# Gate and up expert weights fetched in 8 KB runs, with the normed tokens stored block by block to match

## The chip, the cores and the metric

The kernel runs on one core of one Trainium2 chip. The metric is the device time of one execution in microseconds, the median of several runs. All numbers are float32, or float32r, which is float32 as TensorE reads it in its faster form.

## What is computed

Two transformer blocks in a row work on 256 tokens of width 1024. The first has gated delta-rule attention, differential attention and a dense feed-forward part; the second has a mixer, cross attention to a memory, and a mixture of 32 experts. The change touches the last part alone:

```
h   = rmsnorm(x) * g_moe                       # 256 tokens x 1024
top-1 of 4 groups, top-2 of the 8 experts in it, per token
out = sum over the chosen experts e of  weight[e] * (silu(h @ Wg[e]) * (h @ Wu[e])) @ Wd[e]
x   = rmsnorm(x + out) * g_final
```

Wg and Wu are 1024 x 512 for each expert, Wd is 512 x 1024: 2 MB each, 6 MB for an expert, 192 MB in all. Every expert has 64 slots for tokens. A second pass for experts with more tokens than that lies behind an If at the end.

## The kernel before

**The stage.** Everything up to the router takes some 636 us. Then the expert stage, `moe` (L2045), goes through the 32 experts in 16 pairs. The two experts of a pair sit side by side in halves of TensorE's columns, 64 slots each.

**The weights.** `Experts` (L341) loads the weights on SP's queue in units of 1 MB into slots of 8 KB for each of the 128 partitions. An expert has six units: q = 0 to 3 for gate and up, q = 4 and 5 for down. The order (L347 to 349) is gate and up of pair 0; then, for each p up to 13, gate and up of pair p + 1 and down of pair p; then down of pair 14, gate and up of pair 15, down of pair 15. There are 22 slots: 4 from the time of the first block's feed-forward part (`NRE`), 5 from the time of the cross attention (`NRT`), and 13 more when the buffers of the earlier stages come free (L803). Early on one unit is loaded behind each weight block of the earlier stages (`S.after`, L790 and L795); in `moe` the loads are issued by `X.load` (L2050, L2195, L2212, L2214), as far as slots come free. The list of units goes round the slots, so unit i waits for the last reader of unit i - 22.

**A fetch.** `fetch` (L357) makes a gate/up unit out of two transfers of 512 KB, 256 rows of gate and 256 of up. Partition p takes rows 2p and 2p + 1 of the 256, which lie side by side in memory, 4 KB in one run. A down unit is one transfer of 256 rows of 4 KB; partition p takes rows 2p and 2p + 1, 8 KB in one run.

**The tokens to match.** Since a partition holds rows 2p and 2p + 1, the feature blocks that are multiplied by them are every second feature of 256. `gather` (L2071) multiplies the tokens by one-hot matrices and so collects the tokens of each slot, feature by slot, in `xe`; it reads every second column of x with a step of two (L2079). The columns of `gm`, by which the result is scaled (L2083), are packed in that order on the host (L125). Pair 0 gathers from x itself; the later pairs gather from `xh` and `xl`, two parts of the normed tokens that add up to them (written at L2188 to L2192), four experts at a time.

**The order of a pair.** A turn of the loop (L2198) has: `gather` in even turns; `hid_T`, which transposes the hidden values of pair p; `one_hot`; `gate_up` of pair p + 1; `down` of pair p. `gate_up` (L2097) goes through feature block k, gate or up c, expert j, with one product `mm` (two instructions) for each. Behind the first eight products it calls `between`, which holds `combine` (adds the outputs of pair p - 1 to the tokens) and `slots_T`. `evac` (L2121) takes a pair's output from TensorE's banks, on ACT and VectorE.

```
for k, c, j in [(k, c, j) for k in range(8) for c in range(2) for j in range(n)]:
    if between and (k, c, j) == (2, 0, 0):
        between()
    self.mm(g[c][H[j]], xe[:, k, j0 + j], ws_(j, k // 2)[:, c, k % 2], k == 0, k == 7)
```

**The planner.** In the earlier stages the order of the work is written out by `drive`, which advances the chain that `Pace` (L149) holds to be ready first. `Pace.note` books a transfer by its bytes and an operation by its elements. The router (L1834) is one of the chains. The expert stage is written out by hand.

Of the kernel before, what the change touches and what calls it, by code (L numbers as in the profile page):

```python
# [18 lines left out]
F32 = mybir.dt.float32  # L19
F32R = mybir.dt.float32r  # L20
I32 = mybir.dt.int32
AF = mybir.ActivationFunctionType
ALU = mybir.AluOpType
# [8 lines left out]
CAP = 64  # L32
# [59 lines left out]
def colmajor(v):  # L92
    v = np.asarray(v)
    return v.reshape(-1, 128).T


def pack_small(I):
    g = lambda n: np.asarray(I[n])
    P = Pack()
    P.add("attn_norm", colmajor(g("attn_norm_w")[0]))  # L100
    P.add("ffn_norm", colmajor(g("ffn_norm_w")[0]))
    P.add("g_mix", colmajor(g("g_mix_2")[0]))
    P.add("g_cross", colmajor(g("g_cross_2")[0]))
    P.add("g_moe", colmajor(g("g_moe_2")[0]))
    P.add("g_mem", colmajor(g("g_mem_2")))
    P.add("conv", g("conv_w")[0].reshape(4, 12, 128).transpose(2, 1, 0))
    P.add("la_norm", g("la_norm_w")[0].reshape(128, 1))
    P.add("diff_norm", g("diff_norm_w")[0].reshape(128, 1))
    P.add("gla_norm", g("g_gla_head_2")[0].T)
    P.add("lam_q", np.stack([g("lambda_q1")[0], g("lambda_q2")[0]], 1))  # L110
    P.add("lam_k", np.stack([g("lambda_k1")[0], g("lambda_k2")[0]], 1))
    P.add("a_log", np.broadcast_to(g("a_log")[0], (128, 4)))
    P.add("dt_bias", np.broadcast_to(g("dt_bias")[0], (128, 4)))
    ba = np.zeros((1024, 8), np.float32)
    ba[:] = g("w_in")[0][:, 2048:2056]
    P.add("w_ba", ba.reshape(8, 128, 8).transpose(1, 0, 2))
    P.add("w_alr", g("w_in_2")[0][:, 1536:1552].reshape(8, 128, 16).transpose(1, 0, 2))
    P.add("w_alpha", np.concatenate([g("w_alpha_up_2")[0], g("b_alpha_2")[0][None]], 0))
    rb = np.concatenate([g("rel_bias"), g("rel_bias_2")], 1)
    P.add("rel_bias", np.concatenate([rb, np.ones((1, 12), np.float32)], 0))  # L120
    wr = np.concatenate([g("w_router_group_2")[0], g("w_router_expert_2")[0]], 1)
    P.add("w_rt", wr.reshape(8, 128, 36).transpose(1, 0, 2))
    P.add("b_rt", np.broadcast_to(np.concatenate([g("b_router_group_2")[0], g("b_router_expert_2")[0]]), (128, 36)))
    P.add("final_norm", colmajor(g("final_norm_w")))
    P.add("g_moe_rows", g("g_moe_2")[0].reshape(4, 128, 2).transpose(1, 0, 2))  # L125
    return P


# [141 lines left out]
class Stream:  # L270
# [17 lines left out]
    def load(self, upto=RAW):  # L288
        while self.loaded < len(self.units) and self.loaded < self.freed + upto:
            src, k, n = self.units[self.loaded]  # L290
            w = self.raw[self.loaded % RAW].rearrange("p (k n) -> p k n", n=n)
            src = src.rearrange("(k p) n -> p k n", p=128)
            step = k if self.loaded else 1
            for i in range(0, k, step):
                self.K.nc.sync.dma_start(w[:, i:i + step], src[:, i:i + step])
            self.loaded += 1
            self.after()
# [43 lines left out]
class Experts:  # L341
# [12 lines left out]
        new = [pool.tile([128, 2048], F32, name=f"wm{i}") for i in range(len(order))]  # L354
        self.slots += [new[i] for i in order]

    def fetch(self, slot, e, q, cut=False):  # L357

        nc, I = self.K.nc, self.K.I
        one = (lambda w: w[0, e]) if isinstance(e, int) else (lambda w: w[0, e, :, :].rearrange("o k n -> (o k) n"))  # L360
        rows = lambda n, q: one(I[n])[q * 256:(q + 1) * 256, :].rearrange("(p k) n -> p k n", k=2)
        if q < 4:
            w = slot.rearrange("p (c k n) -> p c k n", k=2, c=2)
            for c, name in enumerate(("w_exp_gate_2", "w_exp_up_2")):
                nc.sync.dma_start(w[:, c], rows(name, q))
        else:
            w = slot.rearrange("p (k n) -> p k n", k=2)
            src = rows("w_exp_down_2", q - 4)
            if cut:
                return w, src  # L370
            nc.sync.dma_start(w, src)
        return w

    def load(self, upto):
        upto = min(upto, len(self.slots)) if self.early else upto
        while self.n < min(upto, len(self.order) - 2):
            self.units[self.order[self.n]] = self.fetch(self.slot(self.n), *self.order[self.n])
            self.n += 1
        if self.n == len(self.order) - 2 and upto >= len(self.order):
            two = [self.fetch(self.slot(self.n + i), *self.order[self.n + i], True) for i in range(2)]  # L380
            for c in range(2):
                for w, src in two:
                    self.K.nc.sync.dma_start(w[:, :, c * 512:c * 512 + 512], src[:, :, c * 512:c * 512 + 512])
            for i, (w, _) in enumerate(two):
                self.units[self.order[self.n + i]] = w
            self.n += 2
# [35 lines left out]
class K:  # L422
# [131 lines left out]
    def rows(self, o, x, k, t, hi, lo, first, last):  # L554
        a = slice(t * 128, (t + 1) * 128)
        self.mm(o, x.hi(k)[:, a], hi, first, False)
        self.mm(o, x.hi(k)[:, a], lo, False, False)
        self.mm(o, x.lo(k)[:, a], hi, False, last)
# [1275 lines left out]
    def router(self, done, ss):  # L1834

        nc = self.nc
        V = nc.vector
        R = self.rt
        self.gm = R.tile([128, 8], F32, name="gm")
        nc.gpsimd.tensor_copy(self.gm, self.small("g_moe_rows"))  # L1840
        hT = [self.g1([128, 2, T], "hT") for _ in range(4)]
        wr = self.small("w_rt").rearrange("p (k n) -> p k n", n=36)
        yield 0
# [2 lines left out]
        for n in range(2):  # L1846
# [3 lines left out]
            for k in range(4 * n, 4 * n + 4, 2):  # L1850
                bank = yield from self.take()
                b = bank.rearrange("p (k n) -> p k n", k=2)
# [82 lines left out]
        while gens[0] or gens[1]:  # L1935
            for i in range(2):
                if gens[i]:
                    try:
# [8 lines left out]
        b = yield from self.take()  # L1947
        strict, one = self.const("strict"), self.ones
# [10 lines left out]
                               op0=ALU.add, op1=ALU.mult)  # L1959
# [85 lines left out]
    def moe(self, A):  # L2045
        tc, nc, I = self.tc, self.nc, self.I
        V = nc.vector
# [3 lines left out]
        x, rk, W32, one_hot, col = self.x, self.rk, self.W32, self.one_hot, self.col  # L2051
        NP = NE // 2
        H = [slice(0, CAP), slice(CAP, 2 * CAP)]
# [5 lines left out]
        xh = [A.tile([128, D], F32R, name=f"xh{t}") for t in range(2)]  # L2059
        xl = [A.tile([128, D], F32R, name=f"xl{t}") for t in range(2)]  # L2060
        xe = self.xe
# [6 lines left out]
                            ranks[:, :, :, None].to_broadcast([128, 2, n, CAP]), op=ALU.is_equal)  # L2068
            return oh

        def gather(n, oh, parts, j0=0, ds=range(8)):  # L2071


            per = 4 if n <= 2 else 2
            for d0 in ds[::per]:
                b = self.bank()[:, :per * n * CAP].rearrange("p (d s) -> p d s", d=per)
                for d in range(per):
                    q, i = (d0 + d) // 2, (d0 + d) % 2
                    mms = [(xs[t][:, q * 256:(q + 1) * 256].rearrange("p (m i) -> p i m", i=2)[:, i], t)  # L2079
                           for t in range(2) for xs in parts]  # L2080
                    for m, (w, t) in enumerate(mms):
                        self.mm(b[:, d], w, oh[:, t, :n].rearrange("p e s -> p (e s)"), m == 0, m == len(mms) - 1)
                V.tensor_tensor(xe[:, d0:d0 + per, j0:j0 + n].rearrange("p d e s -> p d (e s)"), b,  # L2083
                                self.gm[:, d0:d0 + per, None].to_broadcast([128, per, n * CAP]), op=ALU.mult)

        def slots_T(n, pw):

# [9 lines left out]
        def gate_up(n, j0, ws_, between=None):  # L2097

            g = [self.bank() for _ in range(2)]
            for k, c, j in [(k, c, j) for k in range(8) for c in range(2) for j in range(n)]:  # L2100
                if between and (k, c, j) == (2, 0, 0):
                    between()
                self.mm(g[c][H[j]], xe[:, k, j0 + j], ws_(j, k // 2)[:, c, k % 2], k == 0, k == 7)
            sg = self.sg
            R = slice(0, n * CAP)
            nc.scalar.activation(sg[R], g[0][R], AF.Silu)
            V.tensor_tensor(sg[R], g[1][R], sg[R], op=ALU.mult)
            return sg
# [75 lines left out]

        unit = lambda p: (lambda j, q: X.units[2 * p + j, q])
        quad = lambda p: rk[:, :, 2 * p:min(2 * p + 4, NE)]
        gather(2, self.oh, [x])
        for t in range(2):  # L2188
            nc.scalar.activation(xh[t], x[t], AF.Copy, scale=self.r[:, t:t + 1])
        oh = hot(quad(1), 4)  # L2190
        for t in range(2):
            V.scalar_tensor_tensor(xl[t], x[t], self.r[:, t:t + 1], xh[t].bitcast(F32), op0=ALU.mult, op1=ALU.subtract)  # L2192
        hd = gate_up(2, 0, unit(0))
        ys = [[y[:, i] for i in range(2)] for y in (self.c.tile([128, 2, 512], F32R, name=f"ys{c}", tag=f"x{c}") for c in range(2))]
        X.load(8 + NR)  # L2195
# [2 lines left out]
        for p in range(NP - 2):  # L2198
# [4 lines left out]
            if p % 2:  # L2203
                oh = hot(quad(p + 2), min(4, NE - 2 * (p + 2)))
# [11 lines left out]
        p = NP - 2  # L2216
# [20 lines left out]
        with tc.If(most > CAP):  # L2237
            with tc.For_i(0, NE, 1) as e:
                one = bass.ds(e, 1)
# [5 lines left out]
                for _ in range(1, T // CAP):  # L2245
# [4 lines left out]
                    for c in range(2):  # L2250
                        for t in range(2):
                            b = self.bank()
# [34 lines left out]
```

## Time and profile before

| | |
|---|---|
| Runs | 1098.84 us median of three (1098.18 to 1101.12) |
| Profiled execution | 1100.28 us, of it 1098.5 us from the first to the last instruction (the span) |
| Busy share of the span | PE 97%, PEld (weight loads) 68%, DVE 46%, ACT 35%, POOL 5% |
| Chain that ended last, by engine | PE 73%, DMA 21%, DVE 2%, ACT 2%, issue 1% |
| Moved by DMA | 300.06 MB in 106462 packets, mean 273 GB/s |
| Gate, up transfers | 128 each, 512 KB, 10.2 us from issue to landing |
| Down transfers | 62 of 1 MB, 12.6 us, and 4 of 512 KB, 12.7 us |
| Mean granted clock of TensorE | 0.995 |

PE is TensorE, DVE is VectorE, POOL is GpSimd; SP only issues transfers here. A busy PE is not yet a PE at its peak, since matmuls are pipelined and their ends are modelled. The chain of waits is followed back from the last instruction to whatever released each step. All instructions carry one line, L249, that of a helper that records them, so groups are told apart by the names of the tiles: `wm` are the expert slots, `xe` the gathered tokens, `sg` and `hdT` the hidden values, `ys` the outputs of a pair, `ohr` and `oh` the one-hot matrices, `pwT` the matrix that `combine` uses.

### The profile page before, as it was taken

The page shows a single profiled execution, that of the slowest core. Times are in us where ns is not written, and L with a number is a line of the kernel's source. Part 1 is how long each engine was busy: PE and PEld are TensorE (multiplying, and loading weights), DVE is VectorE, ACT ScalarE, POOL GpSimd, SP SyncE. Part 2 cuts the span into 40 slices and gives each one's busy share as a digit, 9 for nine tenths or more (in the row PEclk, how much of TensorE's full clock was granted, in tenths as well). Part 3 has the DMA queues.
Part 4 walks back from the last instruction along what each step waited for, and adds up shares of the span by engine and source line. Part 5 has one row for each costly group of instructions (what it writes and reads, how often), then busy time and mean ns, then how long its engine had stood idle before and what let it go on. Part 6 is the DMA issues. An engine that isn't in the chain of part 4 may idle for free.

```text
span 1098.5 us, 16788 instructions
## 1 busy us (share of the span) xinstructions
PE 1062.1 (97%) x6848; PEld 747.5 (68%) x6848; DVE 504.0 (46%) x917; ACT 381.1 (35%) x678; POOL 57.3 (5%) x85
## 2 busy tenths in 40 slices
PE   9999999999999999999999999999999988989896
PEld 8989788999999888889998753434343434333252
DVE  5777746665655667666576442212121212121021
ACT  6553546644444475566446411000000000000012
POOL 0154011000000010100000000000000000000000
PEclk9999999999999999999999999999999999999998
DMA  8354115576556445454469789999999999999993
GB/s 307 120 190 128 59 66 173 202 271 218 176 170 204 159 136 182 146 178 150 161 217 388 267 314 413 413 414 412 413 414 412 412 412 412 414 412 414 416 413 150
DMA packets 106462, 300.06 MB, mean 273 GB/s; under 512 B 6999, under 2 KB 35980, under 8 KB 98444
## 3 DMA queue, kind: packets, MB, share of 16 engines
q1 hardware_dynamic: 104924, 294.71, 71.3%
q0 software_dynamic: 1024, 3.17, 1.0%
q8 instruction: 56, 0.92, 0.3%
q10 hardware_dynamic: 432, 1.05, 0.3%
q14 instruction: 26, 0.21, 0.1%
HBM read 297.83 MB, written 1.07 MB: 272 GB/s over the span
## 4 chain that ended last, share of the span: by engine, by line
PE 73%; DMA 21%; DVE 2%; ACT 2%; issue 1%; POOL 0%; SPq 0%; ACTq 0%; DVEq 0%
PE bank L249 73%; DMA wm<-in_w_exp_up 13%; DMA wm<-in_w_exp_down 7%; ACT junk L249 1%; DVE cy L249 0%; DMA x<-in_x 0%; DVE junk L249 0%; DVE xTl L249 0%; ACT wh L249 0%; DVE x L249 0%; ACT xTh L249 0%; DVE ys L249 0%; ACT wm L249 0%; ACT ys L249 0%; DVE dp L249 0%
## 5 line engine op out<-in xcount | busy, mean ns | idle before, releaser
L249 DVE TENSOR_TENSOR wl<-wr,wh 128x1024 fp32r<-128x1024 f32 (+1 forms) x175 | 211.1, 1222 | 134.1 <-ACT wh L249 130.8
L249 PE MATMUL bank<-wm,xe 128*64 128x512 f32 x1024 | 230.7, 596 | 3.6 <-DMA wm<-in_w_exp_gate 3.1
L249 PE MATMUL bank<-xTh,wh 128*128 128x256 f32 x768 | 223.3, 291 | 0.0
L249 ACT ACTIVATE wh<-wr 128x1024 fp32r<-128x1024 f32 (+1 forms) x175 | 180.1, 1050 | 118.3 <-PE bank L249 104.6
L249 PE MATMUL bank<-xTl,wh 128*128 128x256 f32 x768 | 217.5, 283 | 0.8 <-DVE xTl L249 0.8
L249 PE MATMUL bank<-xTh,wl 128*128 128x256 f32 x768 | 217.3, 283 | 0.2 <-DVE wl L249 0.2
L249 PEld LDWEIGHTS bank<-wm,xe 128*64 128x64 f32 x1024 | 71.2, 137 | 140.9 <-issue 121.0
L249 PEld LDWEIGHTS bank<-xTh,wh 128*128 128x128 f32 x768 | 147.1, 192 | 4.6 <-issue 2.4
L249 PEld LDWEIGHTS bank<-xTl,wh 128*128 128x128 f32 x768 | 147.2, 192 | 2.3 <-DVE xTl L249 1.2
L249 PEld LDWEIGHTS bank<-xTh,wl 128*128 128x128 f32 x768 | 147.2, 192 | 0.4 <-DVE wl L249 0.4
L249 PE MATMUL bank<-wm,hdT 128*64 128x512 f32 x512 | 123.0, 603 | 14.4 <-DMA wm<-in_w_exp_down 13.7
L249 PEld LDWEIGHTS bank<-wm,hdT 128*64 128x64 f32 x512 | 38.3, 138 | 95.1 <-issue 66.4
L249 ACT ACTIVATE sg<-bank 128x512 f32<-128x512 f32 x20 | 11.9, 597 | 241.9 <-PE bank L249 241.7
L249 DVE TENSOR_TENSOR sg<-bank,sg 128x512 f32<-128x512 f32 x16 | 11.1, 691 | 165.0 <-PE bank L249 165.0
L249 DVE SCALAR_TENSOR_TENSOR ys<-bank,ws,ys 128x512 fp32r<-128x512 f32 x32 | 24.0, 751 | 124.9 <-ACT ys L249 122.9
L249 ACT ACTIVATE ys<-bank,ws 128x512 fp32r<-128x512 f32 x32 | 22.0, 688 | 131.2 <-PE bank L249 131.2
L249 POOL TENSOR_TENSOR nr<-nr,mhalf 128x2 f32<-128x2 f32 (+1 forms) x9 | 6.0, 673 | 681.7 <-DVE nr L249 681.5
L249 PEld LDWEIGHTS bank<-ys,pwT 128*128 128x128 f32 x128 | 22.7, 188 | 18.5 <-issue 11.4
L249 PE MATMUL bank<-wl,fhh 128*128 128x512 f32 x88 | 35.2, 400 | 0.0
L249 PE MATMUL bank<-ys,pwT 128*128 128x512 f32 x128 | 34.6, 410 | 0.6 <-DVE ys L249 0.6
L249 DVE TENSOR_SCALAR pwT<-bank 128x256 fp32r<-128x256 f32 x16 | 6.8, 424 | 61.2 <-PE bank L249 61.2
L249 PE MATMUL bank<-wh,fhh 128*128 128x512 f32 x88 | 34.8, 396 | 0.0
(384 smaller groups left out, 1473.8 us busy)
## 6 DMA issues: line engine op xcount, KB each, us to landing
wm<-in_w_exp_gate SPq DMA_DIRECT2D x128, 512.0 KB, 10.2
wm<-in_w_exp_up SPq DMA_DIRECT2D x128, 512.0 KB, 10.2
wm<-in_w_exp_down SPq DMA_DIRECT2D x62, 1024.0 KB, 12.6
wr<-in_w_in SPq DMA_DIRECT2D x33, 1024.0 KB, 5.2
wr<-in_w_gate_up SPq DMA_DIRECT2D x22, 1024.0 KB, 5.4
wr<-in_w_down SPq DMA_DIRECT2D x11, 1024.0 KB, 5.1
wr<-in_w_out SPq DMA_DIRECT2D x8, 1024.0 KB, 5.1
wr<-in_w_ckv SPq DMA_DIRECT2D x4, 1024.0 KB, 5.8
```

What stands on the lines that cost most here:

```text
L249: r = f(*args, **kw)
```

## The change

A gate/up unit becomes one transfer of 1 MB: q = 0 is 512 rows of gate, q = 1 the same rows of up, q = 2 and 3 the other 512. Partition p takes rows 4p to 4p + 3 of the 512, 8 KB in one run. For experts 0 and 1 (`plain`) a unit holds the same rows in plain order, row k * 128 + p in partition p, four runs of 2 KB. Feature blocks are now every fourth feature of 512; `xh` and `xl` are written in that order, so that the gather reads them, and x for pair 0, block by block without a step. `gm0` holds the plain order of the scale for pair 0. `gate_up` goes through the halves u, then gate or up c, then the four blocks i, then j; `between` is still called at (k, c, j) = (2, 0, 0), which is now behind four products.

```
-    P.add("g_moe_rows", g("g_moe_2")[0].reshape(4, 128, 2).transpose(1, 0, 2))
+    P.add("g_moe_rows", g("g_moe_2")[0].reshape(2, 128, 4).transpose(1, 0, 2))
...
-    def fetch(self, slot, e, q, cut=False):
+    def fetch(self, slot, e, q, cut=False, plain=False):
...
-        rows = lambda n, q: one(I[n])[q * 256:(q + 1) * 256, :].rearrange("(p k) n -> p k n", k=2)
+        rows = lambda n, q, k: one(I[n])[q * 128 * k:(q + 1) * 128 * k, :].rearrange("(p k) n -> p k n", k=k)
         if q < 4:
-            w = slot.rearrange("p (c k n) -> p c k n", k=2, c=2)
-            for c, name in enumerate(("w_exp_gate_2", "w_exp_up_2")):
-                nc.sync.dma_start(w[:, c], rows(name, q))
+            w = slot.rearrange("p (k n) -> p k n", k=4)
+            n = ("w_exp_gate_2", "w_exp_up_2")[q % 2]
+            if plain:
+                nc.sync.dma_start(w, one(I[n])[q // 2 * 512:q // 2 * 512 + 512, :].rearrange("(k p) n -> p k n", p=128))
+            else:
+                nc.sync.dma_start(w, rows(n, q // 2, 4))
         else:
             w = slot.rearrange("p (k n) -> p k n", k=2)
-            src = rows("w_exp_down_2", q - 4)
+            src = rows("w_exp_down_2", q - 4, 2)
...
-            self.units[self.order[self.n]] = self.fetch(self.slot(self.n), *self.order[self.n])
+            self.units[self.order[self.n]] = self.fetch(self.slot(self.n), *self.order[self.n], plain=self.order[self.n][0] < 2)
...
-        self.gm = R.tile([128, 8], F32, name="gm")
+        self.gm, self.gm0 = (R.tile([128, 8], F32, name=n) for n in ("gm", "gm0"))
         nc.gpsimd.tensor_copy(self.gm, self.small("g_moe_rows"))
+        nc.gpsimd.tensor_copy(self.gm0, self.small("g_moe"))
...
+        mixed = lambda w, u: w[:, u * 512:(u + 1) * 512].rearrange("p (m i) -> p i m", i=4)
+        blocks = lambda w, u: w[:, u * 512:(u + 1) * 512].rearrange("p (i m) -> p i m", i=4)
+
+        def gather(n, oh, parts, plain=False):
...
-                    q, i = (d0 + d) // 2, (d0 + d) % 2
-                    mms = [(xs[t][:, q * 256:(q + 1) * 256].rearrange("p (m i) -> p i m", i=2)[:, i], t)
-                           for t in range(2) for xs in parts]
+                    k = d0 + d
+                    mms = [(xs[t][:, k * 128:(k + 1) * 128], t) for t in range(2) for xs in parts]
...
-                                self.gm[:, d0:d0 + per, None].to_broadcast([128, per, n * CAP]), op=ALU.mult)
+                                (self.gm0 if plain else self.gm)[:, d0:d0 + per, None].to_broadcast([128, per, n * CAP]), op=ALU.mult)
...
-            for k, c, j in [(k, c, j) for k in range(8) for c in range(2) for j in range(n)]:
+            for k, c, j in [(4 * u + i, c, j) for u in range(2) for c in range(2) for i in range(4) for j in range(n)]:
                 if between and (k, c, j) == (2, 0, 0):
                     between()
-                self.mm(g[c][H[j]], xe[:, k, j0 + j], ws_(j, k // 2)[:, c, k % 2], k == 0, k == 7)
+                self.mm(g[c][H[j]], xe[:, k, j0 + j], ws_(j, 2 * (k // 4) + c)[:, k % 4], k == 0, k == 7)
...
-        gather(2, self.oh, [x])
+        gather(2, self.oh, [x], True)
         for t in range(2):
-            nc.scalar.activation(xh[t], x[t], AF.Copy, scale=self.r[:, t:t + 1])
+            for u in range(2):
+                nc.scalar.activation(blocks(xh[t], u), mixed(x[t], u), AF.Copy, scale=self.r[:, t:t + 1])
         oh = hot(quad(1), 4)
         for t in range(2):
-            V.scalar_tensor_tensor(xl[t], x[t], self.r[:, t:t + 1], xh[t].bitcast(F32), op0=ALU.mult, op1=ALU.subtract)
+            for u in range(2):
+                V.scalar_tensor_tensor(blocks(xl[t], u), mixed(x[t], u), self.r[:, t:t + 1], blocks(xh[t], u).bitcast(F32),
+                                       op0=ALU.mult, op1=ALU.subtract)
```

## Rows read from the trace of the kernel before

**Rows 1.** The page's 40 slices of 27.5 us: DMA share in tenths, and GB/s.

```profile
DMA  8354115576556445454469789999999999999993
GB/s 307 120 190 128 59 66 173 202 271 218 176 170 204 159 136 182 146 178 150 161 217 388 267 314 413 413 414 412 413 414 412 412 412 412 414 412 414 416 413 150
```

**Rows 2.** Chain of waits from 600 us on: start, us, what.

```profile
636.63 163.84 PE bank L249 x811
...
984.00 10.18 DMA wm<-in_w_exp_up
...
1025.12 15.00 DMA wm<-in_w_exp_down
```

**Rows 3.** Timeline of ACT: the SiLU of two pairs, two apart.

```profile
748.18 0.60 ACT L249 ACTIVATE sg<-bank 128x512 f32<-128x512 f32 x1 [14.89 <-PE bank L249]
...
799.77 0.60 ACT L249 ACTIVATE sg<-bank 128x512 f32<-128x512 f32 x1 [14.89 <-PE bank L249]
```

**Rows 4.** Timeline of SP's queue: issues that follow landings.

```profile
785.40 0.33 SPq L249 DMA_DIRECT2D wm<-in_w_exp_up  x1
...
795.35 0.33 SPq L249 DMA_DIRECT2D wm<-in_w_exp_up  x1
...
805.59 0.33 SPq L249 DMA_DIRECT2D wm<-in_w_exp_up  x1
```

**Rows 5.** Windows: us, busy PE, PEld, DVE, ACT, POOL; clock, DMA share, GB/s.

```profile
10.00:20.00 10.00, 9.09 (x74) 7.84 (x73) 8.71 (x16) 6.81 (x15) 0.00 (x0) 1.00 1.02 352
...
620.00:624.00 4.00, 4.00 (x20) 3.27 (x19) 2.06 (x3) 1.45 (x4) 0.00 (x0) 1.00 0.01 4
641.50:644.00 2.50, 2.50 (x14) 0.86 (x12) 2.50 (x3) 0.00 (x0) 0.00 (x0) 1.00 0.01 3
644.00:650.00 6.00, 6.00 (x30) 2.01 (x28) 0.38 (x1) 0.00 (x0) 0.00 (x0) 1.00 0.87 271
...
704.00:720.00 16.00, 16.00 (x90) 9.13 (x90) 5.79 (x12) 1.45 (x3) 0.00 (x0) 1.00 1.03 409
724.00:730.00 6.00, 6.00 (x30) 2.02 (x28) 0.69 (x1) 0.60 (x1) 0.00 (x0) 1.00 1.02 423
...
1077.70:1081.00 3.30, 3.30 (x10) 0.96 (x8) 0.00 (x0) 0.00 (x0) 0.00 (x0) 0.50 0.42 156
```

**Rows 6.** Timeline of PE around pair 13's down; idle before, releaser in brackets.

```profile
1030.19 2.79 PE L249 MATMUL bank<-wm,xe 128*64 128x512 f32 x10 [0.17 <-DMA wm<-in_w_exp_up]
1032.78 1.04 PE L249 MATMUL bank<-wm,hdT 128*64 128x512 f32 x2
1035.17 3.65 PE L249 MATMUL bank<-wm,hdT 128*64 128x512 f32 x16 [1.35 <-DMA wm<-in_w_exp_down]
1040.16 3.65 PE L249 MATMUL bank<-wm,hdT 128*64 128x512 f32 x14 [1.33 <-DMA wm<-in_w_exp_down]
```

**Rows 7.** Timeline of all engines at the start of the expert stage.

```profile
640.59 13.95 PE L249 MATMUL bank<-wm,xe 128*64 128x512 f32 x64
...
641.91 2.48 DVE L249 SCALAR_TENSOR_TENSOR xl<-x,nr,xh 128x1024 fp32r<-128x1024 f32 x2
...
643.41 0.33 SPq L249 DMA_DIRECT2D wm<-in_w_exp_gate  x1
...
654.48 0.40 PE L249 MATMUL bank<-ohr,xh 128*128 128x256 f32 x1
```

**Rows 8.** PEld groups by form: weight loads, count, busy us, mean ns.

```profile
L249 PEld LDWEIGHTS bank<-xTh,wh 128*128 128x128 f32 x768 | 147.1, 192 | 4.6 <-issue 2.4
...
L249 PEld LDWEIGHTS bank<-ohr,xh 128*128 128x128 f32 x128 | 25.2, 197 | 5.7 <-issue 4.9 <-ACT sg L249 0.8
```

**Rows 9.** Timeline at the last pair's gate and up.

```profile
1057.76 3.60 PE L249 MATMUL bank<-wm,xe 128*64 128x512 f32 x16
...
1057.88 1.65 DVE L249 SCALAR_TENSOR_TENSOR ys<-bank,ws,ys 128x512 fp32r<-128x512 f32 x2 [5.36 <-ACT ys L249]
...
1061.29 1.69 PEld L249 LDWEIGHTS bank<-ys,pwT 128*128 128x128 f32 x8 [0.81 <-issue]
```

More of the change, by code (lines that the diff above doesn't have):

```diff
@@ L2069, in hot @@
             return oh
-        def gather(n, oh, parts, j0=0, ds=range(8)):
+        mixed = lambda w, u: w[:, u * 512:(u + 1) * 512].rearrange("p (m i) -> p i m", i=4)
+        blocks = lambda w, u: w[:, u * 512:(u + 1) * 512].rearrange("p (i m) -> p i m", i=4)
+        def gather(n, oh, parts, plain=False):
             per = 4 if n <= 2 else 2
-            for d0 in ds[::per]:
+            for d0 in range(0, 8, per):
                 b = self.bank()[:, :per * n * CAP].rearrange("p (d s) -> p d s", d=per)
                 for d in range(per):
-                    q, i = (d0 + d) // 2, (d0 + d) % 2
-                    mms = [(xs[t][:, q * 256:(q + 1) * 256].rearrange("p (m i) -> p i m", i=2)[:, i], t)
-                           for t in range(2) for xs in parts]
+                    k = d0 + d
+                    mms = [(xs[t][:, k * 128:(k + 1) * 128], t) for t in range(2) for xs in parts]
                     for m, (w, t) in enumerate(mms):
                         self.mm(b[:, d], w, oh[:, t, :n].rearrange("p e s -> p (e s)"), m == 0, m == len(mms) - 1)
-                V.tensor_tensor(xe[:, d0:d0 + per, j0:j0 + n].rearrange("p d e s -> p d (e s)"), b,
-                                self.gm[:, d0:d0 + per, None].to_broadcast([128, per, n * CAP]), op=ALU.mult)
+                V.tensor_tensor(xe[:, d0:d0 + per, :n].rearrange("p d e s -> p d (e s)"), b,
+                                (self.gm0 if plain else self.gm)[:, d0:d0 + per, None].to_broadcast([128, per, n * CAP]), op=ALU.mult)
         def slots_T(n, pw):
```

## The prediction, made before the change was run

> **What bounds the kernel now.** I read the slices of the page first, for where the DMA engines are full. [rows 1] show that from about the 25th slice to the 39th (650 to 1070 us) they move 412 to 416 GB/s at a busy share of nine tenths or more: this is the expert stage, which streams 192 blocks of 1 MB. TensorE looks just as busy there, so the chain of waits has to decide between the two. In [rows 2] the chain is TensorE up to 800 us, from there a string of weight transfers, each released by the landing of an earlier one, up to 1040.12 (1025.12 + 15.00), and then TensorE to the end. TensorE is thus ahead in the middle and unhindered at the end, and what sets the moment at which the end can begin is the landing of the last down block of pair 13.
>
> That TensorE has room shows in [rows 3]: two pairs of experts, from one SiLU to the second one after it, took 799.77 - 748.18 = 51.6 us while nothing made TensorE wait, or 25.8 us a pair. The transfers need more. [rows 4] give their pace, since an issue on SP follows a landing: the one issued at 984.00 in [rows 2] landed after 10.18 us, eight times 1.27, so eight are under way at a time. Between 785.40 and 795.35 the four issues follow landings of down blocks (1 MB each, runs of 8 KB): 9.95 / 4 = 2.49 us per MB. Between 795.35 and 805.59 the eight issues follow half-blocks of gate and up (512 KB, runs of 4 KB): 10.24 / 8 = 1.28, or 2.56 us per MB. Two windows that hold one kind only say the same: 409 GB/s for gate and up, 423 for down [rows 5]. A pair is 8 x 2.56 + 4 x 2.49 = 30.4 us of transfers against 25.8 us of TensorE. How it ends is in [rows 6]: TensorE waits for gate and up a little (0.17 us at 1030.19), then for two down blocks (1.35 and 1.33 us).
>
> **Run length (fetch).** For experts 2 to 31 a gate or up block becomes one transfer of 1 MB with 8 KB per partition, in shape what a down block is now. I therefore price it by the down rows: 2.56 - 2.49 = 0.075 us per MB (the issues give 0.073, the windows 0.08 with 2.564 and 2.48). How many blocks count: 22 lie in the slots before the stream starts again at 643.41 [rows 7] (pair 0's and pair 1's gate and up, pair 0's down, two of pair 2). Up to pair 13's last down block that leaves 154, of which 6 + 12 x 8 = 102 are gate or up. 102 x 2.56 + 52 x 2.49 = 390.6 us by the pitches, against 1040.12 - 643.41 = 396.7 in the trace; the rest goes to the restart, of which below. The gain is 102 x 0.075 = **7.6 us**. Bounds: 0.09 a block (409 against 423 GB/s, rounded up) gives 9.2; zero if the length of a run buys nothing.
>
> [...]
>
> **TensorE's room.** The new pair would be 12 x 2.49 = 29.8 us of transfers, still above 25.8, so the transfers go on setting the pace and the whole gain arrives at the end of pair 13's down. The last thing that could spoil this is the coarser grain. In an odd pair TensorE now finishes five products (two instructions each, x10) after the last half-block (1030.19 to 1032.78). With whole blocks seven products stand behind the last one; a product is 0.436 us (13.95 us for 32, [rows 7]), so gate/up ends 0.9 us later. The down products then wait until 1035.17 anyway, 2.4 us after 1032.78: covered, at no cost. If that cover were gone it would be 0.9 us once per odd pair while transfers bind, some 3 us.
>
> **Restart of the stream.** The engines stand still from 641.5 to 644 (3 GB/s) and move 271 GB/s from 644 to 650 [rows 5], because every slot is full until TensorE, which began pair 0 at 640.59, frees one [rows 7]. Before, the first half-block is free after 5 products, now the first block after 7: 2 x 0.43 = 0.9 us later. Against that, 1 MB is asked for at once where 512 KB was; the half-rate from 644 to 650 cost 6 x (1 - 271/413) = 2.1 us. Between a loss of 0.9 and a gain of 2.1 I take zero and keep both ends.
>
> **First pair (plain).** Eight blocks now come in runs of 2 KB, as w_in does: a window filled by such loads made 352 GB/s [rows 5], 2.98 us per MB against 2.56, so up to 8 x 0.42 = 3.4 us of transfer time. All are in before the expert stage, and behind them the engines have nothing to do from 620 to 624 (4 GB/s) and again at 641.5, so 6.5 us of idle cover them: zero. Without that cover, 3.4 us. The queue's SP gains issue slots (128 DMAs fewer in all, 0.33 us each), which no one waits for.
>
> **Token gather and splits.** xh and xl are written in four instructions each instead of two, reading x with a step of four elements. The xl ones ended at 644.39 (641.91 + 2.48), the first gather that reads them is at 654.48 [rows 7]: 10 us of cover, against at most a few fixed costs, so zero even at twice the time. The gather's weight loads become contiguous; those with a step of two took 197 ns, contiguous ones of the same size 192 [rows 8]. For the 32 loads of the pair-0 gather that is 0.16 us, for those later less than the transfers hide: zero. One copy on POOL (gm0) comes long before its reader, and the planner books transfers by bytes, so the order it writes out should stay: zero; one more product in its way, 0.43 us, is the bound. The rows of the constants stay the same in size.
>
> **Order in gate_up.** `between` (combine and the transposes of the next slots) now comes after 4 products instead of 8, so 1.7 us earlier. Where it could wait is the last pair: its gate/up begins at 1057.76, and the split of the previous output ends on VectorE at 1057.88 + 1.65 = 1059.53 [rows 9]; 1057.76 + 1.7 = 1059.5. Only the second half of combine reads that last piece, so it costs 0 to 0.1 us; taken as zero. The first two slots of a pair are freed later by what `between` takes, some 2.5 us (combine 2.13 of it), while 10 us of transfers stand in the queue: zero, and see the second rival.
>
> **The tail.** From 1040.12 TensorE runs 58 us to the end of the span and keeps its length, since the blocks for it also land earlier. [...]
>
> **Sum.** -7.6 us. The profiled execution was 1100.28 us around a span of 1098.5; it would be 1092.7. The median of the runs shown is 1.4 us lower, 1098.84, which gives **1091.2 us**.
>
> **Rivals.**
> 1. *The length of a run buys little.* The 2.49 of the down blocks could be a burst after a slow stretch under a ceiling near 413 GB/s, the mean of all slices. For it: the mean hardly moves from slice to slice. Against: the down pitch holds over four landings in a row, and 423 over 6 us. Time: 1098.8, or anything from there down to 1095.5 where a part of it is bought. Chance 0.10. [...]
> 2. *The stream runs out of free slots, ending slower.* The first two slots of a pair come free 2.5 us later. If at that moment less than 1 MB were under way, the engines would idle 2.5 us in each of the nine pairs up to 870 us, before TensorE has caught up: +22 - 7.6, or 1113 us. It decides from one block in flight. Against it: the issues in [rows 4] follow landings, not TensorE, and eight transfers are under way. Chance 0.03.
> 3. *The runs don't become 8 KB.* If each row of 2 KB stayed a packet of its own, 102 x 0.42 = 43 us are lost: 1142 us. Against it: two rows are joined today, and down blocks join two of 4 KB. Chance 0.02.
> 4. *All uncertain ends fall well*: 9.2 + 1.7 + 1.0 = 12 us, 1087. Chance 0.05.
>
> **How the numbers follow.** The forecast has 0.80. Its own range: gain of 5 to 11 us, that is 1088 to 1094; I reach a little further on both sides, 1087 to 1095, which leaves out most of rivals 1 to 4. No-change means within 0.3%, 3.3 us, about what a measurement of this kernel can tell. Faster: forecast and rival 4, 0.85. Same: rival 1, 0.10. Slower: rivals 2 and 3, 0.05.
>
> **What would show it.** Right: transfers of gate and up blocks as 120 issues of 1 MB in place of 240 of 512 KB, landing about 8 x 2.49 = 20 us after issue; SP's issues 2.49 us apart through the whole stage; slices near 420 GB/s; the pair-13 wait near 1032.5 and 58 us from there to the end; TensorE waiting for down blocks still. Wrong: slices still near 413; a DMA share under 0.9 between 650 and 1040; chain steps from TensorE to SP in place of landings; an xl or a combine that TensorE waits for; a first expert product later than 640.6.

## The result, and the profile after

The changed kernel took 1092.16 us, median of six runs (1090.85 to 1092.97), against 1098.87 us for the kernel before: a ratio of 0.9934 with a 95% interval of 0.9921 to 0.9947, so 6.7 us less, between 5.8 and 8.7. The forecast was 1091.2 us, with a range of 1087 to 1095. The profiled execution was 1092.33 us around a span of 1090.5; the one of before, 1100.28, lay 1.4 us above its median, so the two spans differ by 8.0 us and the medians by 6.7.

The page after: span, the 40 slices of DMA share and GB/s, the packets, and the issues of expert weights with their median time from issue to landing. They answer to [rows 1].

```profile
span 1090.5 us, 16590 instructions
...
DMA  8454225576465435463559779999999999999993
GB/s 306 124 192 118 61 77 170 198 270 220 160 201 190 159 117 184 159 198 117 193 193 360 278 306 420 421 422 420 420 421 421 420 422 421 420 420 422 421 421 147
DMA packets 91099, 300.02 MB, mean 275 GB/s; under 512 B 4951, under 2 KB 33932, under 8 KB 67724
...
wm<-in_w_exp_gate SPq DMA_DIRECT2D x64, 1024.0 KB, 19.8
wm<-in_w_exp_up SPq DMA_DIRECT2D x64, 1024.0 KB, 19.8
wm<-in_w_exp_down SPq DMA_DIRECT2D x62, 1024.0 KB, 19.8
```

and the packets on the page before:

```profile
DMA packets 106462, 300.06 MB, mean 273 GB/s; under 512 B 6999, under 2 KB 35980, under 8 KB 98444
```

The slices of the expert stage stood at 412 to 416 GB/s and now stand at 420 to 422, and a block now lands 19.8 us after its issue, eight times 2.48. Packets under 8 KB fell by 98444 - 67724 = 30720, which is 240 transfers times 128 partitions: the two runs of 4 KB have become one of 8 KB. The chain of waits after, which answers to [rows 2]:

```profile
636.73 77.79 PE bank L249 x402
...
714.91 17.64 DMA wm<-in_w_exp_down
...
972.88 19.84 DMA wm<-in_w_exp_up
...
1012.68 19.82 DMA wm<-in_w_exp_down
...
1032.54 2.80 PE bank L249 x11
```

It has the same shape, though it leaves TensorE earlier (714.5 us instead of 800.5): TensorE first, then transfers released by landings, then TensorE. Pair 13's last down block landed at 1012.68 + 19.82 = 1032.50, against 1040.12: **7.62 us earlier**, and 58.0 us are left from there to the end of the span, against 58.4.

SP's queue after, at the restart and in the middle of the stage ([rows 4, 7]), then five windows with the columns of [rows 5]:

```profile
644.17 0.80 SPq L249 DMA_DIRECT2D wm<-in_w_exp_up  x2
...
666.43 0.81 SPq L249 DMA_DIRECT2D wm<-in_w_exp_gate  x2
669.87 0.80 SPq L249 DMA_DIRECT2D wm<-in_w_exp_up  x2
...
745.05 2.82 SPq L249 DMA_DIRECT2D wm<-in_w_exp_gate  x2
...
784.86 2.81 SPq L249 DMA_DIRECT2D wm<-in_w_exp_gate  x2
```

```profile
641.50:645.00 3.50, 3.50 (x20) 1.20 (x18) 3.50 (x4) 0.95 (x1) 0.00 (x0) 1.00 0.00 0
645.00:650.00 5.00, 5.00 (x28) 1.59 (x24) 1.21 (x2) 0.00 (x0) 0.00 (x0) 1.00 0.89 344
650.00:700.00 50.00, 50.00 (x250) 20.39 (x248) 10.24 (x22) 4.26 (x7) 0.00 (x0) 1.00 1.01 423
...
704.00:720.00 16.00, 16.00 (x91) 9.07 (x92) 5.70 (x12) 1.29 (x2) 0.00 (x0) 1.00 1.02 421
724.00:730.00 6.00, 6.00 (x30) 2.01 (x28) 0.69 (x1) 0.00 (x0) 0.00 (x0) 1.00 1.00 418
```

From 745.05 to 784.86 there are 16 issues, blocks of all three matrices: 39.81 / 16 = 2.49 us each, where gate and up had 2.56. The stream starts 0.76 us later than before (644.17 against 643.41). From 0.8 us after its start to 650 us it moves 344 GB/s; the one before moved 271 from 0.6 us after its start to 650. Early in the stage the issues are not 2.49 us apart: at 666.43 and 669.87 two come at once, 3.44 us apart, about the time of eight products, which free two slots. The engines stay full all the same (423 GB/s from 650 to 700).

TensorE around pair 13's down after, beside [rows 6]:

```profile
1022.60 3.22 PE L249 MATMUL bank<-wm,xe 128*64 128x512 f32 x13 [1.12 <-DMA wm<-in_w_exp_up]
...
1027.57 3.65 PE L249 MATMUL bank<-wm,hdT 128*64 128x512 f32 x16 [1.32 <-DMA wm<-in_w_exp_down]
1032.54 3.65 PE L249 MATMUL bank<-wm,hdT 128*64 128x512 f32 x14 [1.32 <-DMA wm<-in_w_exp_down]
```

The wait for the last up block has grown from 0.17 to 1.12 us, seven products (thirteen of their instructions are in the trace) stand behind it instead of five, and the down blocks are waited for as before.

### The profile page after: what moved, and what is told of

Same layout as the page of the kernel before. It is cut to its first block, busy times and chain, and to the rows that moved or that the text cites. A ratio compares the mean times of both kernels' runs of the same rounds, so it can differ in the third digit from the quotient of the medians.

```text
span 1090.5 us, 16590 instructions
## 1 busy us (share of the span) xinstructions
PE 1057.4 (97%) x6848; PEld 750.2 (69%) x6848; DVE 505.7 (46%) x919; ACT 383.7 (35%) x680; POOL 57.5 (5%) x86
## 2 busy tenths in 40 slices
DMA packets 91099, 300.02 MB, mean 275 GB/s; under 512 B 4951, under 2 KB 33932, under 8 KB 67724
## 3 DMA queue, kind: packets, MB, share of 16 engines
q0 software_dynamic: 1024, 3.17, 1.0%
## 4 chain that ended last, share of the span: by engine, by line
PE 64%; DMA 29%; DVE 2%; ACT 2%; issue 1%; POOL 0%; SPq 0%; ACTq 0%; DVEq 0%
PE bank L249 64%; DMA wm<-in_w_exp_up 18%; DMA wm<-in_w_exp_down 11%; ACT junk L249 1%; DVE cy L249 0%; DMA x<-in_x 0%; DVE junk L249 0%; DVE xTl L249 0%; ACT wh L249 0%; DVE x L249 0%; ACT xTh L249 0%; DVE ys L249 0%; ACT wm L249 0%; ACT ys L249 0%; DVE dp L249 0%
## 5 line engine op out<-in xcount | busy, mean ns | idle before, releaser
L249 PEld LDWEIGHTS bank<-wm,xe 128*64 128x64 f32 x1024 | 74.9, 137 | 137.1 <-issue 122.0
L249 PE MATMUL bank<-wh,fhl 128*128 128x512 f32 x88 | 34.5, 392 | 0.0
## 6 DMA issues: line engine op xcount, KB each, us to landing
wm<-in_w_exp_gate SPq DMA_DIRECT2D x64, 1024.0 KB, 19.8
wm<-in_w_exp_up SPq DMA_DIRECT2D x64, 1024.0 KB, 19.8
wm<-in_w_exp_down SPq DMA_DIRECT2D x62, 1024.0 KB, 19.8
```

Source lines behind the costliest of these rows:

```text
L249: r = f(*args, **kw)
```

## The experiments

All times are medians. Ratios are to the kernel before, run beside each kernel on the same chip, where it had 1099.5 to 1100.5 us.

**Run length alone.** A block stays one transfer, but in two runs of 4 KB for each partition; the order of the tokens is made to match.

```
-                nc.sync.dma_start(w, rows(n, q // 2, 4))
+                nc.sync.dma_start(w.rearrange("p (h k) n -> p h k n", h=2),
+                                  one(I[n])[q // 2 * 512:q // 2 * 512 + 512, :].rearrange("(h p k) n -> p h k n", h=2, k=2))
```

> Changed kernel, but a gate or up block of 1 MB comes in runs of 4 KB (two runs for each partition), tokens stored to match; still one transfer for a block. Theory A (each run costs the DMA engines a fixed time, so run length alone makes the gain): the pitch of gate and up blocks goes back from 2.49 to 2.56 us per MB, 102 blocks x 0.073 = 7.4 us slower than the changed kernel, 1099 to 1100 us, slices near 413 GB/s again. Rival B (half as many transfers make the gain, through their issues and receipts): no change from the changed kernel, 1092 us, 421 GB/s.

1100.0 us, ratio 1.0004 (0.9995 to 1.0013): the whole gain is gone. Two steps of the chain, two pairs apart, and the slices:

```profile
928.98 20.06 DMA wm<-in_w_exp_down
...
989.75 20.11 DMA wm<-in_w_exp_down
```

```profile
GB/s 303 123 191 118 63 73 173 197 266 229 166 180 194 159 135 180 160 173 147 161 210 386 271 313 414 413 413 413 413 413 412 413 413 412 413 413 414 416 412 170
```

Two pairs took 60.77 us; less 8 down blocks of 2.49, 16 gate and up blocks took 40.85, or 2.55 us each. Theory A holds and B falls: with half as many transfers and runs of 4 KB the old pace is back.

**Half-size transfers in 4 KB runs.** The order of the products, splits and first pair stay as changed.

```
-                nc.sync.dma_start(w, rows(n, q // 2, 4))
+                for h in range(2):
+                    nc.sync.dma_start(w[:, 2 * h:2 * h + 2], rows(n, q // 2, 4)[:, 2 * h:2 * h + 2])
```

> Changed kernel, but each gate or up block comes in two transfers of 512 KB, each half of the block's rows in a partition, so in runs of 4 KB, with the order of the products as changed. Both theories: 1099 us. What it tells apart is the rest of the change: if order, splits and first pair cost nothing, it stands within 1 us of the kernel before; if they gave or cost anything, it is off by that.

1100.35 us, ratio 1.0003 (0.9993 to 1.0012), so with the old transfers all the rest of the change together is worth nothing that the medians can tell, to within some 1 us. The chain of its profiled execution is a little longer; pair 13's last down block:

```profile
1026.77 14.96 DMA wm<-in_w_exp_down
```

It lands at 1041.73, 1.6 us later than before, of which 0.35 is a later start of the stage. So the rest of the change gives none of the 7.6 us, and may cost about 1 us in this form.

**Half-size transfers in 8 KB runs**, by halves of the partitions.

```
-                nc.sync.dma_start(w, rows(n, q // 2, 4))
+                for h in range(2):
+                    P = slice(64 * h, 64 * h + 64)
+                    nc.sync.dma_start(w[P], rows(n, q // 2, 4)[P])
```

> Changed kernel, but each gate or up block comes in two transfers of 512 KB, partitions 0 to 63 and 64 to 127, in runs of 8 KB. Theory A (run length): 1092 us, pitch still 2.49 us per MB, as long as a transfer to 64 partitions keeps all 16 engines busy; if it doesn't, the DMA share of the stage falls under 0.9 and the run tells nothing. Rival B (number of transfers): back to 1099 us and 413 GB/s.

1424.47 us, ratio 1.284 (1.277 to 1.291): neither theory's number. A window of its trace, with the columns of [rows 5]:

```profile
700.00:750.00 50.00, 37.77 (x156) 15.95 (x154) 6.43 (x13) 2.57 (x4) 0.00 (x0) 0.89 1.02 276
```

The engines were busy (a share of 1.02) and the page counts about as many packets as in the changed kernel, 93021 against 91099, but they moved 276 GB/s, where the changed kernel moved 420 in the same window at a share of 1.01: a packet took longer. So a block fetched as two transfers of 64 partitions is far slower; why, no run here shows. On A against B, which the two runs above had settled, it says nothing.

**Runs of 2 KB everywhere.**

```
-            if plain:
+            if True:
```

(with `mixed` and `g_moe_rows` in plain order too)

> Changed kernel, but all gate and up blocks in plain order, four runs of 2 KB for each partition, one transfer of 1 MB. Theory A with a fixed cost for each run: from 8 to 4 KB the pitch rose by 0.073 us per MB for 128 runs more, so 2 KB (256 runs more again) gives 2.49 + 0.22 = 2.71 us per MB, 102 x 0.22 = 22 us slower than the changed kernel, 1114 us. By the window of 352 GB/s of the kernel before (2.98 us per MB) it would be 50 us slower, 1142 us. Rival B (number of transfers): 1092 us.

1116.32 us, ratio 1.0151 (1.013 to 1.0173), so 16.8 us slower than the kernel before and some 24 slower than the changed one, where 22 were expected from a fixed cost for each run and 50 from the window of 352 GB/s. The chain, two pairs apart:

```profile
945.88 20.72 DMA wm<-in_w_exp_gate
...
1009.17 20.60 DMA wm<-in_w_exp_gate
```

63.29 - 8 x 2.49 = 43.37 us for 16 blocks: 2.71 us, the expected figure. The pitches for 8, 4 and 2 KB are thus 2.49, 2.55 and 2.71 us per MB. A block has 128 runs more at 4 KB and 256 more again at 2 KB; by an estimate from the pitches, with the runs spread evenly over the 16 engines of the page, that makes 8 and 10 ns for a run.

**More work for TensorE.** Ten more products (float32r, 512 columns, results unused) in each of the turns 0 to 12.

```
+            if p < 13:
+                b = self.bank()
+                for _ in range(10):
+                    self.mm(b, xh[0][:, :128], xh[0][:, :512], True, True)
             hdT = hid_T(2, hd)
```

> Changed kernel with 10 more float32r products of 512 columns in each of the turns 0 to 12 of the expert loop (some 2.6 us of TensorE each, 34 us in all; results unused). Theory A (transfers set the pace, TensorE has 29.9 - 25.8 = 4.1 us of room in a pair): no change within 1 us, 1092 us, TensorE's waits for down blocks shrink. Rival C (TensorE sets the pace, its waits are only grain): up to 34 us slower, 1126 us.

1098.32 us, ratio 0.9983 (0.9974 to 0.9993): about 5 us slower than the changed kernel, neither 0 nor 34. The added products (their group: count, busy us, mean ns) and the chain:

```profile
L249 PE MATMUL bank<-xh 128*128 128x512 f32 x130 | 32.8, 398 | 0.0
```

```profile
636.78 405.30 PE bank L249 x1978
...
1043.68 31.95 PE bank L249 x171
```

The chain is TensorE from start to end, so its room is used up. The added products of one turn and what follows them:

```profile
658.31 2.48 PE L249 MATMUL bank<-xh 128*128 128x512 f32 x10
660.62 0.63 PE L249 MATMUL bank<-cst,sg 128*128 128x128 f32 x4
```

From start to start they push TensorE's work back by 2.31 us here and by 2.42 in odd turns, some 31 us in all; the 32.8 above counts the overlap with their neighbours too. The step that begins at 1043.68 began at 1036.94 in the changed kernel: of 31 us, 6.7 came through and 24 were absorbed. The room is real, but it is 24 us up to pair 13, not 13 times 4.1. The likely reason, which no run isolates: the stream enters the stage 22 blocks ahead, and TensorE spends most of its surplus in using those up. Theory A is right on what sets the pace in the changed kernel, and its number was wrong.

**First pair in 8 KB runs too.**

```
-            self.units[self.order[self.n]] = self.fetch(self.slot(self.n), *self.order[self.n], plain=self.order[self.n][0] < 2)
+            self.units[self.order[self.n]] = self.fetch(self.slot(self.n), *self.order[self.n])
...
-                    mms = [(xs[t][:, k * 128:(k + 1) * 128], t) for t in range(2) for xs in parts]
+                    mms = [(mixed(xs[t], k // 4)[:, k % 4] if plain else xs[t][:, k * 128:(k + 1) * 128], t) for t in range(2) for xs in parts]
```

> Changed kernel with the first pair in runs of 8 KB too; its gather then reads x with a step of four elements, and the plain scale is not used. Theory A (the first pair's loads are hidden behind idle engines, and a step in the weight load costs little): within 1 us of the changed kernel, 1092 us; the pair-0 gather of 32 products stays near 4.04 us. Rival D (the plain order is part of the gain): slower by the gather's longer weight loads, up to 4 us if they take twice as long.

1095.15 us, ratio 0.9955 (0.9941 to 0.9968). Its interval just overlaps the changed kernel's; the trace decides. Pair 0's gather and its weight loads (group: count, busy us, mean ns), the restart on SP and pair 13's last down block in the chain, in this kernel:

```profile
636.78 7.73 PE L249 MATMUL bank<-oh,x 128*128 128x128 f32 x32 [0.29 <-ACT cut L249]
```

```profile
L249 PEld LDWEIGHTS bank<-oh,x 128*128 128x128 f32 x32 | 7.5, 329 | 0.4 <-ACT cut L249 0.4
```

```profile
648.12 0.80 SPq L249 DMA_DIRECT2D wm<-in_w_exp_up  x2
```

```profile
1016.85 19.80 DMA wm<-in_w_exp_down
```

and the same gather in the changed kernel:

```profile
636.73 3.84 PE L249 MATMUL bank<-oh,x 128*128 128x128 f32 x32 [0.29 <-ACT cut L249]
```

Read with a step of four floats, a weight load takes 329 ns instead of the 192 of a contiguous one [rows 8], the gather 7.73 us instead of 3.84, and the stream restarts 4 us later. Pair 13's last down block lands at 1036.65 instead of 1032.50, so the delay comes through to the end of the transfers. Rival D is right: the plain order of the first pair keeps some 4 us that the longer runs would otherwise cost. The medians show less of it, 2 to 3 us. In the two profiled executions the ends of the spans differ by 2.8: the last down products took 7.11 us in this one and 8.81 in the changed kernel's, which has a stretch at a granted clock of 0.50 there (last section).

**Products by expert**, to free a slot sooner and have less left behind the last landing.

```
-            for k, c, j in [(4 * u + i, c, j) for u in range(2) for c in range(2) for i in range(4) for j in range(n)]:
-                if between and (k, c, j) == (2, 0, 0):
+            for k, c, j in [(4 * u + i, c, j) for u in range(2) for c in range(2) for j in range(n) for i in range(4)]:
+                if between and (k, c, j) == (0, 0, 1):
...
+            jkc = [(j, 2 * q + i, c) for q in range(2) for j in range(n) for i in range(2) for c in range(2)]
```

> Changed kernel with the products of one block done together: in gate_up the expert j outside the four blocks i, in down each expert's two blocks k and both halves c together; between is still called behind four products. Theory A: the first slot comes free after 4 products instead of 7, so the stream starts 3 x 0.436 = 1.3 us earlier, and after pair 13's last down block 4 products are left instead of 7, which brings the end 1.3 us nearer; 2.6 us faster than the changed kernel, 1089.5 us. Rival E (TensorE needs the two column halves in turn, so its pace falls when one half comes four times in a row): products slower than 0.436 us, no gain or a loss.

1131.86 us, ratio 1.0284 (1.027 to 1.0298): 31 us slower than before, as Rival E had it. The gate and up products between 660 us and 1060 us (group: count, busy us, mean ns), then those of the changed kernel from 660 to 860:

```profile
L249 PE MATMUL bank<-wm,xe 128*64 128x512 f32 x886 | 248.1, 598 | 0.0
```

```profile
L249 PE MATMUL bank<-wm,xe 128*64 128x512 f32 x508 | 112.5, 595 | 0.0
```

248.1 / 886 = 0.280 us an instruction against 112.5 / 508 = 0.221. TensorE became the bound: in this run the chain is TensorE alone from 636.64 to 1069.70. The first issue came at 644.09, hardly earlier than 644.17, which no run here explains.

**The last gather in TensorE's wait.** Two places for it, with the changed kernel run again beside them. Ahead of pair 13's down:

```
             X.load(12 * p + 16 + NR)
+            if p == NP - 3:
+                gather(2, oh, [xh, xl])
             down(2, hdT, unit(p))
...
         pT = slots_T(2, pw)
-        gather(2, oh, [xh, xl])
```

or ahead of pair 14's gate/up, with the one-hot matrix made a turn earlier:

```
+            if p == NP - 4:
+                oh = hot(quad(NP - 1), 2)
+            if p == NP - 3:
+                gather(2, oh, [xh, xl])
...
-        gather(2, oh, [xh, xl])
```

> The changed kernel itself, for a ratio on the same chip as the two that follow: 0.9934 of the kernel before, within 0.0013.

> Changed kernel with the last gather (pair 15, 32 products, some 3.9 us) moved from behind pair 13's down to before it, where TensorE waits for down blocks. Theory A (transfers set the pace up to pair 13's last down block, TensorE alone after it): TensorE would end gate/up at 1025.7, gather to 1029.6, and 16 down products of 7.05 us to 1036.6 instead of 1036.2, so the way to the end is 3.9 - 0.4 = 3.5 us shorter, 1088.7 us. Rival C (TensorE sets the pace throughout): no change, 1092 us.

> As the one before, but the last gather stands ahead of pair 14's gate/up, with its one-hot matrix made one turn earlier, so that TensorE's wait for the last up block (1.12 us) is filled too. Theory A: 0.4 us less than the one before, 1088.3 us, TensorE's three waits in that turn gone or nearly. Rival C: 1092 us.

The changed kernel took 1091.43 us, ratio 0.9928 (0.9914 to 0.9941). The first place gave 1090.49, 0.9923 (0.991 to 0.9937), the second 1092.12, 0.9928 (0.9914 to 0.9941): neither gains what was expected, and none can be told from the changed kernel. TensorE in the first of them:

```profile
1029.76 7.09 PE L249 MATMUL bank<-wm,hdT 128*64 128x512 f32 x32
...
1040.66 7.09 PE L249 MATMUL bank<-wm,hdT 128*64 128x512 f32 x32 [0.52 <-ACT hdT L249]
...
1062.28 3.65 PE L249 MATMUL bank<-wm,xe 128*64 128x512 f32 x14 [0.96 <-DMA wm<-in_w_exp_up]
1065.86 2.05 PE L249 MATMUL bank<-g,cst 8*128 8x128 f32 x16
```

and the second and fourth of these steps in the changed kernel beside it:

```profile
1043.25 7.09 PE L249 MATMUL bank<-wm,hdT 128*64 128x512 f32 x32
...
1066.42 2.05 PE L249 MATMUL bank<-g,cst 8*128 8x128 f32 x16
```

The step itself went as expected: pair 13's down ran 16 products without a wait, to 1036.8. But of the 3.5 us TensorE was only 2.6 ahead at pair 14's down (1040.66 against 1043.25), where it waited for ACT, and 0.6 behind the last gate and up (1065.86 against 1066.42), where the last up block of pair 15 landed only at 1062.28. Theory A had the transfers out of the way from 1032.5 on; in truth they stay close ahead of TensorE to the end, so that TensorE, once early, meets them. The spans were 1088.5 against 1089.0 for the changed kernel beside it, so some 0.5 us of the 3.5 was left. The second place met the same landing: there TensorE waits 1.11 us for it at 1062.23.

## Why the prediction was right

- **Run length: right, in mechanism and size.** The term was 7.6 us, 102 blocks at 0.075. Measured at the place where the chain turns, pair 13's last landing, it is 7.62: 102 x (2.56 - 2.49) = 7.1 to 7.4 from the pitches, 0.76 lost and, as the rest of the sum, a little more than that won at the restart. The two 4 KB runs put the whole gain on the length. By the estimate from the measured pitches a run takes 8 to 10 ns on an engine. Rival 1, that a run of this length buys little, fell with it.
- **The median** fell by 6.7 and, beside the last experiments, by 8.2 us; 7.6 lies in both intervals. Executions differ by the granted clock too, by 1.7 us in the two profiles of the last section.
- **Restart: zero, right**, 0.76 us later against a faster start (344 GB/s against 271). The number of issues and the time to landing came out as foretold (transfers of 1 MB, 19.8 us); their spacing of 2.49 us did so only from some 720 us on.
- **Rivals 2 and 3** did not come. By their spacing the early issues did wait for freed slots, which the second rival feared, but the engines stayed full (423 GB/s). The runs became 8 KB, as the packets show (30720 fewer under 8 KB). The price of the third, 43 us by the window of 352 GB/s, was too high: with runs of 2 KB everywhere the kernel was 16.8 us slower than before, and the 3.4 us of the first pair, from the same window, would by the measured pitches be 8 x 0.16 = 1.3.
- **Coarser grain: right.** Seven products after the last block of gate and up, and still a wait of 1.32 us for the down blocks at 1027.57.
- **Splits: covered, as said, with the price at the edge of what I allowed.** I counted fixed costs, at worst twice the time. They took about twice the time. After and before:

```profile
L249 ACT ACTIVATE xh<-x,nr x4: 1212/1218/1224, 636.6 to 639.9; 128x512 fp32r<-128x512 f32 x4
L249 DVE SCALAR_TENSOR_TENSOR xl<-x,nr,xh x4: 1156/1176/1180, 641.8 to 645.0; 128x512 fp32r<-128x512 f32 x4
```

```profile
L249 ACT ACTIVATE xh<-x,nr x2: 1139/1144/1148, 636.5 to 637.8; 128x1024 fp32r<-128x1024 f32 x2
L249 DVE SCALAR_TENSOR_TENSOR xl<-x,nr,xh x2: 1279/1279/1279, 641.9 to 643.1; 128x1024 fp32r<-128x1024 f32 x2
```

  (count; shortest, median and longest ns; first and last start.) On VectorE 1.18 us for half the elements, where a whole instruction took 1.28. They end by 646.2; the gather needs them at 654.4.
- **First pair: the transfers are hidden, as said, but the step's worth was missed.** I priced only the loads and called the gather's weight loads nearly free by a row with a step of two [rows 8]. Without `plain` the step would be four, and that costs 3.9 us in the gather. The sum holds because the change has `plain`.
- **TensorE's room:** "still above 25.8, so the transfers go on setting the pace" is right; the total room, 24 us, I had not worked out, and the expectation of the run with more products failed by it.
- **The tail:** kept its length, 58.0 us, and in the profiled execution its stretch at a granted clock of 0.50. That the 1.7 us of rival 4 come with the change, no run shows: the changed kernel has the stretch in one profile and not in the other, and its last down products took 8.81 and 7.11 us there (last section). "Unhindered at the end" was true by a small margin only: that the transfers stand so close to TensorE there, I had not seen; the moved gather showed it.

## What to carry to other kernels

Where the DMA engines are full for long, the length of a contiguous run can count, as it did here (2.56 us per MB in runs of 4 KB, 2.49 in runs of 8 KB): price it from a stream of the longer runs in the same trace, block for block, and follow it to the one landing at which the chain turns. When a layout is changed for the transfers, look at every reader that then steps through memory, and leave contiguous the one that nothing covers (here pair 0's gather, 3.84 us against 7.73). Before work is moved into a wait, look one transfer further: the next landing may leave hardly more room (here 0.5 us of the 3.5 was left).

## What was not expected of the hardware

- **A step of four floats took 1.7 to 2.1 times the time for an element on three engines**, by the whole time of the instructions. TensorE's weight load took 329 against 192 ns, ACT 1.22 us for 512 elements against 1.14 for 1024 contiguous ones, VectorE 1.18 for 512 against 1.28 for 1024; a step of two cost a weight load 197 against 192. Why four costs so much more than two, no run here shows.
- **Products that take turns between the column halves** ran at 0.221 us an instruction, four products in a row in one half at 0.280; which part of the chip sets this, no run here shows.
- **Two transfers of 64 partitions in place of one of 128** made the kernel 1.28 times as long, at 276 GB/s between 700 and 750 us with the engines busy.
- **The clock near the end differs between executions of one kernel.** The last down products in the chain and a window in them (columns of [rows 5], the clock third from the end), in the profile of the changed kernel and in that of its second run:

```profile
1069.56 8.81 PE bank L249 x32
...
1070.00:1072.00 2.00, 2.00 (x6) 0.49 (x4) 0.00 (x0) 0.00 (x0) 0.00 (x0) 0.50 0.50 188
```

```profile
1069.83 7.11 PE bank L249 x32
...
1070.00:1073.00 3.00, 3.00 (x16) 1.00 (x16) 0.00 (x0) 0.00 (x0) 0.00 (x0) 1.00 0.40 150
```

The 1.7 us between them are a stretch at a granted clock of 0.50 in the first, as at 1077.7 before [rows 5]; the second has none, and a span of 1089.0 instead of 1090.5. The kernel is the same, and what decides between the two, no run here shows.
